# Masking the turned probabilities of sliding-window attention: one VectorE instruction into one tile instead of two into two

## The chip, the cores and the metric

One core of a Trainium2 chip runs one program. The metric is the device time of one execution, in microseconds (us); shown are the median and the spread of three executions, and one further execution that was profiled. In the profile PE is the engine of matmuls and PEld its loading of weights, DVE is VectorE, ACT is ScalarE, POOL is GpSimd and SP issues the transfers.

## What is computed

A decoder trunk of two layers, for 1024 prompt tokens and 64 sample tokens of width 1024: a gated-MLP token mixer, then grouped-query attention over a sliding window of 128 tokens with a sink per head, and behind each a SwiGLU feed-forward part. The change lies in the attention of the prompt alone:

```python
def swa_prompt(q, k, v, sinks):            # blocks of 128 queries, 16 heads, 2 key heads, 64 wide
    kk = concatenate([previous block of k, own block of k])        # 256 keys per block
    band = (kpos <= qpos) & (qpos - kpos < WINDOW)
    valid = band & ((block > 0) | (kpos >= WINDOW))
    scores = einsum('bnqkgd,bnskd->bnkgqs', qb, kk) * HEAD_DIM ** -0.5
    scores = where(valid, scores, -inf)
    probs = sink_softmax(scores, sinks)
    out = einsum('bnkgqs,bnskd->bnqkgd', probs, vv)
```

Of a query's 256 keys exactly 128 are in its window: key j of its own block if j is not behind the query, else key j of the block before. So the kernel keeps 128 scores per query, and separates the two kinds only when the probabilities meet the values.

## The kernel before

The program is one stream of matmuls with everything else beside it. The feed-forward parts and projections are products in two halves of precision: an operand is split into a high part (ACT copies it, lines 391 and 635) and a low part (DVE subtracts, lines 392 and 636), and three matmuls take the place of one (lines 629 to 631, 1000 to 1002, 1368 to 1370).

The attention stands between the first layer's feed-forward part and the output projection. It works in 32 **units**, one for a pair of heads f (0 to 7) and a pair of blocks n0 (0, 2, 4, 6). A unit goes through these steps:

- **scores** (lines 2292 to 2314): PE multiplies queries and keys (2302, 2303) into two PSUM banks; ACT copies the own block's scores into a tile `sc` (2306, 2309) and DVE writes the previous block's over it where the window wants them (2307, 2310). There are four buffers of `sc`, and five PSUM banks called `bank`.
- **softmax** (lines 2184 to 2194): POOL puts the sink beside the scores (2187), DVE finds the maximum (2188, 2189), ACT takes exponents (2191), DVE the reciprocal (2193), POOL scales (2194).
- **turn** (line 2211): PE transposes the unit's four 128x128 squares into one PSUM buffer `aux` (three of these).
- **probs** (lines 2316 to 2325): DVE multiplies the turned squares by the mask `mcT` of the own block into half of an `act` tile (2319), and then by the mask `mpT` of the previous block back into `sc` (2321). For two of the 32 units (by the bits of `K["mp"]`) ACT copies the squares and POOL masks them instead (2323, 2324).
- **weigh** (lines 2327 to 2340): PE multiplies values and probabilities into another `aux` buffer. For each of the four squares comes a matmul with the own block's values (2335), which reads the first product, and one with the previous block's (2337), which reads the second. A unit has 8 matmuls, or 6 where n0 is 0. They are float32 and use 64 of the array's 128 columns, so the profile gives them as 128*64 and shows two records for each. All other matmuls around them are 128*128. In the trace's names `aux<-act,act` of line 2335 and `aux<-sc,act` of line 2337 are these two kinds.

Between the units stand the products of the queries (lines 629 to 631, called Q below), and later the first parts of the output projection (lines 1000 to 1002, called C below), which also need the attention's rows split by lines 635 and 636 (`convert`).

Python code records the steps with due times (`flow.later`, with the delays in `K`), but that is not the last word: the tile framework is built with `schedule_with_timeline_sim=True`, and puts each engine's instructions in the order in which its own simulated timeline finds them ready. So the length and the readiness that it assumes for an instruction decide what stands beside what on every engine. On the chip each engine keeps that order and waits on semaphores.

Of the kernel before, what the change touches and what calls it, by code (L numbers as in the profile page):

```python
# [12 lines left out]
BF16 = mybir.dt.bfloat16  # L13
I32 = mybir.dt.int32
AF = mybir.ActivationFunctionType
ALU = mybir.AluOpType
# [3 lines left out]
P = 128  # L20
# [15 lines left out]
HN = 512  # L36
# [23 lines left out]
K = {'sown': 2500, 'sprobs': 8460, 'sweigh': 1107, 'xrows': 1607, 'tokw': 17761, 'var': 4147, 'centre': 4050, 'lnfin': 5018, 'mix0': 4469, 'mixc': 1659, 'mixn': 7044, 'mixt': 988, 'ln0': 1571, 'lnc': 6100, 'krow': 92, 'vrow': 2056, 'probs': 10000, 'weigh': 556, 'beg': 73, 'beg0': 0, 'ql': [159, 251], 'mp': [191, 253, 255, 255], 'ustep': 1.65, 'sat': [19, 31], 'cst0': 3015, 'cstep': 306, 'guest': [4, 7], 'lns': 47, 'sturn': 1300, 'rops': 9500, 'rstep': 550, 'zsum': 1500}  # L60
# [155 lines left out]
def trunk_kernel(ctx, tc, a):  # L216
    nc = tc.nc
    flow = Flow()
    count = [0]

    def mk(pool, shape, dt, tag, **kw):
        count[0] += 1
        return pool.tile(shape, dt, tag=tag, name=f"{tag}_{count[0]}", **kw)

    cpool = ctx.enter_context(tc.tile_pool(name="cpool", bufs=1))
# [6 lines left out]
    def act_tile(dt=F32):  # L232
        return mk(apool, [P, T], dt, "act")
# [4 lines left out]
    def bank():  # L238
        return mk(psum, [P, 512], F32, "bank", bufs=5)
# [39 lines left out]
    def tmp(shape=None, dt=F32, tag="tmp", **kw):  # L279
        return mk(ph.t, shape or [P, HN], dt, tag, **kw)  # L280
# [4 lines left out]

    pm_i = mk(cpool, [P, P], I32, "pmi")

    mcT, mpT = mk(cpool, [P, P], BF16, "mcT"), mk(cpool, [P, P], BF16, "mpT")

    def window_masks():  # L290
        m, m2 = tmp([P, P]), tmp([P, P])
# [11 lines left out]
    class Samples:  # L303
# [41 lines left out]
        def probs(self, sc):  # L345
            p4 = turn(sc)
            ptc, ptn = sc, half_quad()
            nc.vector.tensor_tensor(ptc, p4, kpS[:, None, :].to_broadcast([P, 4, P]), op=ALU.mult)
            nc.vector.tensor_tensor(ptn[:DS], p4[:DS], nwS[:DS, None, :].to_broadcast([DS, 4, P]), op=ALU.mult)
            flow.later(K["sweigh"], lambda: self.weigh(ptc, ptn))  # L350

        def weigh(self, ptc, ptn):

            halves = []
            for hb in range(2):
                ps = bank()
                for e in range(2):
                    j, out = 2 * hb + e, ps[:, e * 256:(e + 1) * 256]
                    v, vn = (t[:, 4 * hb:4 * hb + 4, :].rearrange("p b d -> p (b d)") for t in (self.cv, self.vnew))
                    nc.tensor.matmul(out, ptc[:, j, :], v, start=True, stop=False)  # L360
                    nc.tensor.matmul(out, ptn[:DS, j, :], vn, start=False, stop=True)
                own = tmp([P, P])
                for b in range(4):
                    r = slice(b * 32, (b + 1) * 32)
                    nc.scalar.activation(own[r, :].rearrange("p (e d) -> p e d", e=2),
                                         ps[r, :].rearrange("p (e b d) -> p e b d", e=2, b=4)[:, :, b, :], AF.Copy)
                halves.append(own)
            flow.pe(2000)
            W.done(self.slot)
            flow.later(K["sown"], lambda: self.features(halves))  # L370
# [1827 lines left out]
    def half_quad():  # L2198

        if not halves:  # L2200
            t = act_tile()
            halves.extend(t[:, i * HN:(i + 1) * HN] for i in range(2))
        return halves.pop(0).rearrange("p (q j) -> p q j", q=4)
# [4 lines left out]
    def turn(sc):  # L2208
        ps = aux()
        for j in range(4):  # L2210
            nc.tensor.transpose(ps[:, j * P:(j + 1) * P], sc[:, j, :], ident)
        flow.pe(440)
        return ps.rearrange("p (q j) -> p q j", q=4)
# [78 lines left out]
    def scores(f, n0):  # L2292
        kv = f // 4
        scw = quad("sc", 4)
        sc = scw[:, :, :P]
        for i in range(2):
            n = n0 + i
            ps = bank().rearrange("p (e j) -> p e j", e=2)
            k0 = max(n - 1, 0) * P
            for e in range(2):  # L2300
                q = S[f][e][:, n * P:(n + 1) * P]
                nc.tensor.matmul(ps[:, e, :], q, kk[kv][0][:, k0:k0 + 256], start=True, stop=False)
                nc.tensor.matmul(ps[:, e, :], q, kk[kv][1][:, k0:k0 + 256], start=False, stop=True)
            sv = sc[:, 2 * i:2 * i + 2, :]
            if n:
                nc.scalar.activation(sv, ps[:, :, P:], AF.Copy)
                nc.vector.copy_predicated(sv, pm_i[:, None, :].to_broadcast([P, 2, P]), ps[:, :, :P])
            else:
                nc.scalar.activation(sv, ps[:, :, :P], AF.Copy)
                nc.vector.copy_predicated(sv, pm_i[:, None, :].to_broadcast([P, 2, P]),  # L2310
                                          neg[:, None, :].to_broadcast([P, 2, P]))
        flow.pe(900)
        softmax(scw, sinkq[:, f].rearrange("p i e -> p (i e)"), 4)
        flow.later(K["probs"], lambda: probs(f, n0, sc))

    def probs(f, n0, sc):
        p4 = turn(sc)
        pc = half_quad()
        nc.vector.tensor_tensor(pc, p4, mcT[:, None, :].to_broadcast([P, 4, P]), op=ALU.mult)
        if K["mp"][n0 // 2] >> f & 1:  # L2320
            nc.vector.tensor_tensor(sc, p4, mpT[:, None, :].to_broadcast([P, 4, P]), op=ALU.mult)
        else:
            nc.scalar.activation(sc, p4, AF.Copy)
            nc.gpsimd.tensor_tensor(sc, sc, mpT[:, None, :].to_broadcast([P, 4, P]), op=ALU.mult)
        flow.later(K["weigh"], lambda: weigh(f, n0, sc, pc))

    def weigh(f, n0, pp, pc):
        kv = f // 4
# [45 lines left out]
    for st in range(4 * KD):  # L2374
        f, s = divmod(st, 4)
# [72 lines left out]
```

## Time and profile before

| | |
|---|---|
| median of three executions | 2109.6 us (2109.23 to 2111.39) |
| the profiled execution | 2105.51 us |
| its span, first to last instruction | 2103.8 us |
| mean granted TensorE clock | 0.999 |
| attention units on the trace | 1113 us (first turn) to 1294 us (last weigh) |

The page counts busy time by engine over the span; the view by windows does the same for a stretch. Records of matmuls overlap, since a new one starts before the last has ended: the pace of PE is read from the distance between starts in the timeline, not from a record's length. The view of waits names for each idle time of an engine the instruction that ended it.

### The profile page before, as it was taken

How to read it: one execution, taken by the hardware profiler on the slowest of the kernel's cores; microseconds unless marked ns; L12 is line 12 of the kernel's file. 1: busy time of each engine (PE TensorE's matmuls, PEld its weight loads, DVE VectorE, ACT ScalarE, POOL GpSimd, SP SyncE). 2: the span in 40 equal slices, each digit the busy share in tenths (PEclk: the TensorE clock that was granted, in tenths of full speed). 3: DMA queues.
4: the chain of work that ended last, by engine and by line, in shares of the span. 5: the costliest groups of instructions: out<-in, count | busy, mean ns of one | idle time of the engine just before them, and what ended most of it. 6: DMA issues, size and time to landing. Idle time of an engine off the chain costs nothing.

```text
span 2103.8 us, 29105 instructions
## 1 busy us (share of the span) xinstructions
PE 2076.8 (99%) x10890; PEld 1781.2 (85%) x10890; DVE 1357.5 (65%) x2141; ACT 1042.4 (50%) x2078; POOL 180.0 (9%) x259
## 2 busy tenths in 40 slices
PE   8999999999999999999999999999999999999998
PEld 8999888888888888888898887888888888888886
DVE  5565467665656675676767776576666666665676
ACT  6245556544444443534576665565444544344342
POOL 2422210000000000000114331110000000000000
PEclk9999999999999999999999999999999999999999
DMA  6211332332232338767442212423232323277574
GB/s 235 80 41 32 102 130 67 96 98 90 97 98 90 95 121 287 244 192 232 123 131 55 54 31 67 145 79 96 82 103 97 102 77 108 87 274 259 180 247 150
DMA packets 161312, 261.56 MB, mean 124 GB/s; under 512 B 21009, under 2 KB 86673, under 8 KB 161170
## 3 DMA queue, kind: packets, MB, share of 16 engines
q1 hardware_dynamic: 161170, 259.69, 38.0%
q8 instruction: 86, 1.41, 0.3%
q14 instruction: 56, 0.46, 0.1%
HBM read 193.42 MB, written 60.62 MB: 121 GB/s over the span
## 4 chain that ended last, share of the span: by engine, by line
PE 93%; DVE 4%; ACT 1%; DMA 1%; issue 1%; POOL 0%; SPq 0%; DVEq 0%; POOLq 0%; ACTq 0%
PE bank L1594 14%; PE bank L1368 13%; PE bank L1369 13%; PE bank L1370 13%; PE bank L629 5%; PE bank L630 5%; PE bank L631 5%; PE aux L1594 4%; PE bank L1000 3%; PE bank L1002 3%; PE bank L1001 3%; PE bank L1448 2%; PE bank L1447 2%; PE aux L1602 2%; PE aux L1101 1%; PE aux L914 1%
## 5 line engine op out<-in xcount | busy, mean ns | idle before, releaser
L1368 PE MATMUL bank<-act,act 128*128 128x512 f32 x1232 | 485.0, 394 | 1.8 <-ACT act L1776 1.8
L1369 PE MATMUL bank<-act,act 128*128 128x512 f32 x1232 | 482.3, 391 | 0.0
L1370 PE MATMUL bank<-act,act 128*128 128x512 f32 x1232 | 479.5, 389 | 0.0
L1594 PE MATMUL bank<-act,act 128*128 128x512 f32 x1452 | 341.2, 389 | 0.0
L1594 PEld LDWEIGHTS bank<-act,act 128*128 128x128 f32 x1452 | 272.4, 188 | 56.5
L392 DVE TENSOR_TENSOR act<-raw,act 128x1024 fp32r<-128x1024 f32 x186 | 228.1, 1229 | 123.2 <-ACT act L391 113.5
L391 ACT ACTIVATE act<-raw 128x1024 fp32r<-128x1024 f32 x186 | 196.5, 1058 | 207.8 <-PE bank L1448 67.5
L1370 PEld LDWEIGHTS bank<-act,act 128*128 128x128 f32 x1232 | 231.4, 188 | 48.8
L1368 PEld LDWEIGHTS bank<-act,act 128*128 128x128 f32 x1232 | 231.6, 188 | 47.8 <-ACT act L1776 2.7
L1369 PEld LDWEIGHTS bank<-act,act 128*128 128x128 f32 x1232 | 231.7, 188 | 43.2
L635 ACT ACTIVATE act<-act 128x1024 fp32r<-128x1024 f32 (+5 forms) x207 | 163.8, 837 | 178.9 <-PE bank L1594 69.8
L636 DVE TENSOR_TENSOR act<-act,act 128x1024 fp32r<-128x1024 f32 (+5 forms) x207 | 190.3, 958 | 42.0 <-ACT act L635 30.8
L629 PE MATMUL bank<-act,act 128*128 128x384 f32 (+1 forms) x624 | 208.7, 335 | 8.5 <-ACT act L522 8.5
L630 PE MATMUL bank<-act,act 128*128 128x384 f32 (+1 forms) x624 | 205.4, 330 | 0.7 <-DVE tok L973 0.7
L631 PE MATMUL bank<-act,act 128*128 128x384 f32 (+1 forms) x624 | 205.6, 330 | 0.0
L485 ACT ACTIVATE raw<-raw,vcol 128x256 f32<-128x256 f32 x352 | 151.9, 498 | 69.4 <-DMA raw<-in_f_w_up 43.8
L978 POOL TENSOR_TENSOR tok<-tok,expo 128x1 f32<-128x1 f32 (+1 forms) x63 | 39.0, 619 | 1587.5 <-DVE tok L973 1587.5
L629 PEld LDWEIGHTS bank<-act,act 128*128 128x128 f32 x624 | 118.1, 189 | 10.3 <-ACT act L522 8.5
L630 PEld LDWEIGHTS bank<-act,act 128*128 128x128 f32 x624 | 118.1, 189 | 2.0 <-issue 1.0
L631 PEld LDWEIGHTS bank<-act,act 128*128 128x128 f32 x624 | 118.0, 189 | 0.9 <-issue 0.9
L1000 PE MATMUL bank<-act,act 128*128 128x512 f32 x256 | 100.9, 397 | 1.9 <-DVE sc L339 1.5
L1001 PE MATMUL bank<-act,act 128*128 128x512 f32 x256 | 100.1, 392 | 0.0
(280 smaller groups left out, 3094.6 us busy)
## 6 DMA issues: line engine op xcount, KB each, us to landing
act<-in_f_w_down SPq DMA_DIRECT2D x90, 512.0 KB
raw<-in_f_w_gate SPq DMA_DIRECT2D x44, 512.0 KB
raw<-in_f_w_up SPq DMA_DIRECT2D x44, 512.0 KB
act<-hid_s SPq DMA_DIRECT2D x40, 512.0 KB
rows<-stream SPq DMA_DIRECT2D x24, 512.0 KB
hid_x<-rows SPq DMA_DIRECT2D x44, 256.0 KB
hid_s<-act SPq DMA_DIRECT2D x44, 256.0 KB
hid_s<-rows SPq DMA_DIRECT2D x44, 256.0 KB
```

Source lines behind the costliest of these rows:

```text
L391: nc.scalar.activation(self.hi, raw, AF.Copy)
L392: nc.vector.tensor_tensor(self.lo, raw, self.hi.bitcast(F32), op=ALU.subtract)
L629: nc.tensor.matmul(out[:, :n], h, xh[:, cs:cs + n], start=begin, stop=False)
L630: nc.tensor.matmul(out[:, :n], h, xl[:, cs:cs + n], start=False, stop=False)
L631: nc.tensor.matmul(out[:, :n], l, xh[:, cs:cs + n], start=False, stop=end)
L635: nc.scalar.activation(hi, src, AF.Copy)
L636: nc.vector.tensor_tensor(lo, src, hi.bitcast(F32), op=ALU.subtract)
L1000: nc.tensor.matmul(ps[:m, :], xh, h, start=begins and j == 0, stop=False)
L1368: nc.tensor.matmul(ps, h, xh, start=begin and k == 0, stop=False, skip_group_check=not begin)
L1369: nc.tensor.matmul(ps, h, xl, start=False, stop=False, skip_group_check=not begin)
L1370: nc.tensor.matmul(ps, l, xh, start=False, stop=k == 3, skip_group_check=not begin)
L1594: nc.tensor.matmul(ps, x, w, start=begin and e == k == 0, stop=end and e == n - 1 and k == 2, skip_group_check=adds)
```

## The change

The two masks become two halves of one tile `mcp`; `mcT` and `mpT` are views of it. In `probs`, one DVE instruction reads the turned squares twice (a broadcast over a dimension of two), multiplies them by both masks, and writes 1024 elements per partition into one `act` tile `both`. `weigh` then reads both operands from that tile. The branch with ACT and POOL is gone, and `sc` has no reader or writer behind the turn.

```diff
-    mcT, mpT = mk(cpool, [P, P], BF16, "mcT"), mk(cpool, [P, P], BF16, "mpT")
+    mcp = mk(cpool, [P, 2, P], BF16, "mcp")
+    mcT, mpT = mcp[:, 0, :], mcp[:, 1, :]
...
     def probs(f, n0, sc):
         p4 = turn(sc)
-        pc = half_quad()
-        nc.vector.tensor_tensor(pc, p4, mcT[:, None, :].to_broadcast([P, 4, P]), op=ALU.mult)
-        if K["mp"][n0 // 2] >> f & 1:
-            nc.vector.tensor_tensor(sc, p4, mpT[:, None, :].to_broadcast([P, 4, P]), op=ALU.mult)
-        else:
-            nc.scalar.activation(sc, p4, AF.Copy)
-            nc.gpsimd.tensor_tensor(sc, sc, mpT[:, None, :].to_broadcast([P, 4, P]), op=ALU.mult)
-        flow.later(K["weigh"], lambda: weigh(f, n0, sc, pc))
+        both = act_tile()[:, :2 * HN].rearrange("p (s q j) -> p s q j", s=2, q=4)
+        nc.vector.tensor_tensor(both, p4[:, None].to_broadcast([P, 2, 4, P]), mcp[:, :, None, :].to_broadcast([P, 2, 4, P]),
+                                op=ALU.mult)
+        flow.later(K["weigh"], lambda: weigh(f, n0, both[:, 1], both[:, 0]))
```

In the changed file the lines up to `probs` have a number higher by one, and those behind it a number lower by three: the new instruction is line 2320, the matmuls of weigh are lines 2332 and 2334, the turn is 2212.

The framework gives nearly all of the attention another order. Three places show how.

PE, the fourth unit (its output is `aux_9933` before and `aux_9930` after; `bank_9998` and `bank_9994` hold the same product of queries). Before:

```order
L631 MATMUL bank_9998<-act_8873,act_9522 128x384
L2335 MATMUL aux_9933<-act_9895,act_9378 64x128
L629 MATMUL bank_9998<-act_8942,act_9521 128x384
L630 MATMUL bank_9998<-act_8943,act_9521 128x384
L631 MATMUL bank_9998<-act_8942,act_9522 128x384
L629 MATMUL bank_9998<-act_8967,act_9521 128x384
L2337 MATMUL aux_9933<-sc_9683,act_9378 64x128
L2335 MATMUL aux_9933<-act_9895,act_9378 64x128
L2337 MATMUL aux_9933<-sc_9683,act_9378 64x128
L2335 MATMUL aux_9933<-act_9895,act_9378 64x128
L2337 MATMUL aux_9933<-sc_9683,act_9378 64x128
L2335 MATMUL aux_9933<-act_9895,act_9378 64x128
```

After:

```order
L632 MATMUL bank_9994<-act_8941,act_9521 128x384
L2212 MATMUL aux_9895<-ident_71,sc_9710 128x128 x4
L2332 MATMUL aux_9930<-act_9893,act_9377 64x128
L2334 MATMUL aux_9930<-act_9893,act_9377 64x128
L2332 MATMUL aux_9930<-act_9893,act_9377 64x128
L2334 MATMUL aux_9930<-act_9893,act_9377 64x128
L2332 MATMUL aux_9930<-act_9893,act_9377 64x128
L2334 MATMUL aux_9930<-act_9893,act_9377 64x128
L2332 MATMUL aux_9930<-act_9893,act_9377 64x128
L2334 MATMUL aux_9930<-act_9893,act_9377 64x128
L630 MATMUL bank_9994<-act_8966,act_9520 128x384
```

Before, one matmul of the unit (own block) goes ahead, four of the queries follow, and then come the other seven; after, the eight stand together. Over the whole order of PE the 240 matmuls of weigh stand in 46 runs before and in 30 after; before, 18 of the 32 units are cut in two (13 times into 1 and 7, five times into 3 and 3, and none is after).

DVE, near the end of the attention. Line 339 (340 after) writes a part of the samples' scores and releases a bank; lines 636 (637 after) with `act<-act` are the low parts of the conversions. Before:

```order
L636 TENSOR_TENSOR act_11766<-aux_11757,act_11766 128x256
L636 TENSOR_TENSOR act_11775<-act_10327,act_11775 128x256
L636 TENSOR_TENSOR act_11775<-act_10659,act_11775 128x256
L636 TENSOR_TENSOR act_11789<-act_9878,act_11789 128x256
L636 TENSOR_TENSOR act_11792<-act_9878,act_11792 128x64
L636 TENSOR_TENSOR act_11789<-act_9996,act_11789 128x256
L636 TENSOR_TENSOR act_11792<-act_9996,act_11792 128x64
L636 TENSOR_TENSOR act_11799<-act_10327,act_11799 128x256
L636 TENSOR_TENSOR act_11792<-act_10327,act_11792 128x64
L636 TENSOR_TENSOR act_11799<-act_10659,act_11799 128x256
L636 TENSOR_TENSOR act_11792<-act_10659,act_11792 128x64
L339 COPY_PREDICATED sc_11853<-nsi_10060,bank_11855 128x4x8
```

After:

```order
L637 TENSOR_TENSOR act_11691<-aux_11682,act_11691 128x256
L2320 TENSOR_TENSOR act_11706<-aux_11701,mcp_87 128x1024
L340 COPY_PREDICATED sc_11836<-nsi_10056,bank_11838 128x4x8
L637 TENSOR_TENSOR act_11708<-act_9876,act_11708 128x256
L637 TENSOR_TENSOR act_11711<-act_9876,act_11711 128x128
L637 TENSOR_TENSOR act_11708<-act_9992,act_11708 128x256
L637 TENSOR_TENSOR act_11711<-act_9992,act_11711 128x128
```

Line 339 stood behind all the conversions before, and now stands ahead of them; the last scores' line 2307 goes the other way, behind them.

PE, the last units but one. Each reads what DVE makes of the turn (line 2211, or 2212 after) of its own unit: `act_11958` after is made from `aux_11953`. After:

```order
L2334 MATMUL aux_11928<-act_11919,act_9377 64x128
L2212 MATMUL aux_11953<-ident_71,sc_11795 128x128 x4
L2332 MATMUL aux_11960<-act_11958,act_9377 64x128
L2334 MATMUL aux_11960<-act_11958,act_9377 64x128
L2332 MATMUL aux_11960<-act_11958,act_9377 64x128
```

Before, seven matmuls of another unit stood between these two steps:

```order
L2335 MATMUL aux_11946<-act_11936,act_9378 64x128
L2211 MATMUL aux_11971<-ident_71,sc_11812 128x128 x4
L2337 MATMUL aux_11946<-sc_11670,act_9378 64x128
L2335 MATMUL aux_11946<-act_11936,act_9378 64x128
L2337 MATMUL aux_11946<-sc_11670,act_9378 64x128
L2335 MATMUL aux_11946<-act_11936,act_9378 64x128
L2337 MATMUL aux_11946<-sc_11670,act_9378 64x128
L2335 MATMUL aux_11946<-act_11936,act_9378 64x128
L2337 MATMUL aux_11946<-sc_11670,act_9378 64x128
L2335 MATMUL aux_11978<-act_11936,act_9378 64x128
```

So after the change this one unit's weigh follows its turn directly.

## The prediction

> **What bounds the kernel.** First the page: busy time by engine, and the chain that ended last.
>
> ```profile
> PE 2076.8 (99%) x10890; PEld 1781.2 (85%) x10890; DVE 1357.5 (65%) x2141; ACT 1042.4 (50%) x2078; POOL 180.0 (9%) x259
> ...
> PE 93%; DVE 4%; ACT 1%; DMA 1%; issue 1%; POOL 0%; SPq 0%; DVEq 0%; POOLq 0%; ACTq 0%
> ```
>
> PE is busy nearly always and holds 93% of the chain. So an instruction less on DVE, ACT or POOL is worth nothing by itself. The change can move the time in two ways only: by the idle time of PE in the attention, and by the PE time that the order of its matmuls costs. The first is bounded by the view of PE's waits from 1100 to 1340 us (total, times, longest):
>
> ```profile
> PE bank L1000 <- DVE sc L339: 1.5, 1, 1.5
> PE aux L2211 <- POOL sc L2194: 1.4, 2, 0.9
> PE aux L2335 <- ACT tmp L1991: 0.8, 1, 0.8
> PE aux L2335 <- DVE act L2319: 0.7, 1, 0.7
> PE bank L1000 <- ACT act L391: 0.4, 1, 0.4
> ```
>
> These five sum to 4.8 us. That is all that shorter waits could ever bring; only the 1.5 us of line 2335 is a wait for the product that the change merges (at the 0.8 us too, which the view gives to line 1991, the matmul's real operand is line 2319's). The next view, by windows (length, then busy time of PE, PEld, DVE, ACT, POOL), shows where DVE could become the limit:
>
> ```profile
> 1120.00:1200.00 80.00, 78.39 (x626) 69.19 (x626) 59.42 (x141) 54.78 (x201) 27.38 (x40) 1.00 0.16 44
> 1260.00:1280.00 20.00, 17.80 (x185) 13.67 (x184) 19.59 (x60) 14.82 (x56) 5.24 (x6) 1.00 0.19 62
> ```
>
> Over most of the attention DVE has a quarter of its time free; from 1260 to 1280, where the conversions of the attention's rows come, it is full, and PE loses 2.2 us there.
>
> **The second way: what a visit to weigh costs PE.** The timeline of PE at the fourth unit, which is cut into one matmul and seven:
>
> ```profile
> 1130.29 0.34 PE L631 MATMUL bank<-act,act 128*128 128x384 f32 x1
> 1130.56 0.43 PE L2335 MATMUL aux<-act,act 128*64 128x128 f32 x2
> 1130.92 0.45 PE L629 MATMUL bank<-act,act 128*128 128x384 f32 x1
> ...
> 1131.38 0.35 PE L631 MATMUL bank<-act,act 128*128 128x384 f32 x1
> 1131.56 0.34 PE L629 MATMUL bank<-act,act 128*128 128x384 f32 x1
> 1131.83 0.32 PE L2337 MATMUL aux<-sc,act 128*64 128x128 f32 x1
> ...
> 1132.86 0.44 PE L630 MATMUL bank<-act,act 128*128 128x384 f32 x1
> ```
>
> Two matmuls of the queries start 0.18 us apart (1131.38, 1131.56). With one matmul of weigh between, two start 1130.92 - 1130.29 = 0.63 us apart: that visit costs 0.45 us. The other seven cost 1132.86 - 1131.56 - 0.18 = 1.12 us. Together 1.57. Against it a unit whose eight stand together:
>
> ```profile
> 1293.03 0.40 PE L1000 MATMUL bank<-act,act 128*128 128x512 f32 x1
> 1293.26 0.40 PE L1001 MATMUL bank<-act,act 128*128 128x512 f32 x1
> 1293.59 0.45 PE L2335 MATMUL aux<-act,act 128*64 128x128 f32 x4
> ...
> 1294.66 0.50 PE L1002 MATMUL bank<-act,act 128*128 128x512 f32 x1
> ```
>
> Here the starts lie 1.40 us apart where 0.23 would do: 1.17 us for the whole unit. So the cut costs 1.57 - 1.17 = **0.40 us**. From the two pieces alone: twelve more records (two per matmul) cost 1.12 - 0.45 = 0.67 us, 0.056 each, and so a visit has a fixed part of 0.45 - 0.11 = 0.34 us. Both say that PE pays for going to weigh and back, not only for the matmuls. I take 0.40, since it compares a whole unit with a cut one.
>
> The Trainium skill, page "TensorEngine Tiling (Array Packing)", section Key Properties, states that a change of tiling mode drains TensorE. By that rule the price belongs to each change between 128*128 and 128*64, whatever the neighbour; without it the price of a cut would be nothing and the gain below would shrink to the waits. The fixed 0.34 us in the rows speaks for the rule.
>
> **The change, part by part.**
>
> - *Order of PE.* The new order has the 240 matmuls of weigh in 30 visits and not in 46, since both operands come ready at once. PE does 16 visits less: 16 x 0.40 = 6.4 us (5.4 with 0.34). PE is the limit nearly everywhere here, so it counts in full, but for about one unit in the full stretch of DVE. Nothing is added on PE.
> - *DVE.* The prices, from DVE's own timeline:
>
> ```profile
> 1264.26 1.22 DVE L392 TENSOR_TENSOR act<-raw,act 128x1024 fp32r<-128x1024 f32 x1
> 1265.39 0.44 DVE L2307 COPY_PREDICATED sc<-pmi,bank 128x256 f32<-128x256 int32 x1
> ...
> 1272.28 0.68 DVE L2319 TENSOR_TENSOR act<-aux,mcT 128x512 f32<-128x512 f32 x1
> 1272.88 0.67 DVE L2321 TENSOR_TENSOR sc<-aux,mpT 128x512 f32<-128x512 f32 x1
> 1273.48 0.76 DVE L2307 COPY_PREDICATED sc<-pmi,bank 128x256 f32<-128x256 int32 x2
> ...
> 1274.47 2.62 DVE L636 TENSOR_TENSOR act<-act,act 128x256 fp32r<-128x256 f32 x10
> 1277.02 0.19 DVE L339 COPY_PREDICATED sc<-nsi,bank 128x32 f32<-128x32 int32 x1
> ```
>
>   The pair holds DVE for 1.20 us (1272.28 to 1273.48). No row has 1024 elements out of PSUM; line 392 has 1024 out of SBUF and holds DVE for 1.13 us (1264.26 to 1265.39). Bounds: 1.13, and 2.4 us if it went at half that pace. I take 1.13, since line 2319 already reads PSUM and a broadcast mask at the pace of its size. DVE then gives up 30 x 0.07 = 2.1 us and takes on 2 x 0.53 = 1.1 for the two units that ACT and POOL shared; off the path, hidden by DVE's free quarter. What ACT and POOL lose lies beside PE too.
> - *The added wait.* Weigh's first matmul needed 0.68 us of DVE before and needs 1.22 now; its second operand comes 0.06 us earlier (0.60 + 0.68 before). The whole of PE is queued behind that first matmul. In the new order I counted PE's work between each unit's turn and its weigh at the spacings above: the shortest are 0, 1.5, 1.6, 2.0, 2.1, 2.3 and 2.3 us, the rest 2.7 or more. How long DVE needs from the turn on:
>
> ```profile
> 1283.30 0.60 PE L2211 MATMUL aux<-ident,sc 128*128 128x128 f32 x4
> ...
> 1283.93 0.69 DVE L2319 TENSOR_TENSOR act<-aux,mcT 128x512 f32<-128x512 f32 x1 [0.90 <-PE aux L2211]
> ```
>
>   From the turn's first matmul 0.63 us to DVE's start, then 1.22; the turn holds PE for some 0.6 of it. So a distance of 1.3 us suffices when DVE is free. Only the unit with 0 waits for certain: **+1.3 us**, and the last one, behind lines 348 and 349, about +0.2.
> - *Waits that go.* The 0.8 and the 0.7 us of line 2335: all other units have distance enough now (-1.5). The 1.5 us of line 339: it stood behind ten conversions (2.62 us), and now stands ahead. The next late thing is line 2307 of the last scores, which has gone behind them, and whose bank the next product of the projection needs. From line 2320 of the unit ahead, DVE has to do some 12.1 us until then (conversions at 0.26 each, the rest by the rows above) and PE 11.7, so some 0.5 us stays (-1.0). One of the two waits for POOL, 0.5 us: `sc` now comes free with the turn, so the next scores run further ahead (-0.5).
> - *SP.* Two weight loads move behind more of the small shifts of line 1977. They go to tiles that are read tens of us later; I cost this at nothing.
>
> Waits: +1.5 - 3.0 = -1.5. A new order may bring waits I don't see, so I take -1.0. **Sum: -6.4 - 1.0 = -7.4 us.** Against the profiled execution (2105.5) that gives 2098.1; the executions shown have a median 4.1 us above it, and I carry the difference: 2109.6 - 7.4 = **2102.2 us**.
>
> **Rivals.**
>
> - *DVE becomes the bound.* For it: 19.59 of 20 us busy from 1260 on, and the distances of 1.5 to 2.1 us don't hold if two more instructions of 0.6 us stand ahead on DVE (then 2.5 us are needed, not 1.3). The wait for line 339 stays whole (no gain), those four units wait some 2.6 us in all, and the visits saved in the full stretch (0.8) don't count: 6.4 - 0.8 - (1.5 + 2.6) + (1.5 + 0.5) = 3.5 us gained, 2106.1. Against it: DVE's load doesn't grow.
> - *The visits cost nothing that returns.* If the fixed part were only the matmuls' start that later work makes up, just the waits change: 2108.6. Against it: two separate pieces give 0.34.
> - *Slower: the merged instruction is slow.* One mechanism: two broadcasts out of PSUM, with POOL at work beside it. A DVE row that is stretched exists, line 2052; line 2319 in the same place is not (minimum, median, maximum in ns):
>
> ```profile
> L2052 DVE TENSOR_TENSOR tmp<-tmp,act x30: 472/556/1928, 1099.6 to 1260.9; 64x384 fp32r<-64x384 f32 x21, 64x320 fp32r<-64x320 f32 x9
> ...
> L2319 DVE TENSOR_TENSOR act<-aux,mcT x32: 658/690/693, 1119.0 to 1291.6; 128x512 f32<-128x512 f32 x32
> ```
>
>   At 2.4 us each, a unit needs a distance of 2.5 us: the seven below it wait 4.4 us more, three or four in DVE's full stretch add 4.2, and DVE's extra 32 x 1.2 us would take most of its free quarter, which I put at 2.0 us of further waits: -7.4 + 10.6 = 3.2 us slower, 2112.8. It outweighs the gain from about 2 us on. Line 2319's narrow spread speaks against it.
>
> **How the numbers follow.** What a measurement of this kernel can tell from no change is about 0.2%, 4.2 us. The forecast (gain of 4.2 to 11) gets 0.75; DVE as the bound 0.14 and visits without a price 0.06, both within 0.2%; slower 0.05. So faster 0.75, same 0.20, slower 0.05. The range goes down to a gain of 11 us (16 x 0.42 and nearly all waits gone), 2098.6, and up to a gain of 2 (between the first two rivals), 2107.6.
>
> **What would show it.** In the profile of the changed kernel: weigh's records in runs of 12 or 16, at 1.17 us a unit with no lone pair; the merged instruction at 1.22 us with little spread; PE's waits in the attention at 3 to 5 us, the largest at the last unit but one and at the first product behind the conversions; the stage from the first turn to the first product of the second half shorter by about 7 us, and everything behind it moved by as much. A merged instruction over 2 us, or waits over 8 us, would make the prediction wrong.

## The result, and the profile after

| | before | after |
|---|---|---|
| median of six runs, us | 2109.4 | 2098.1 |
| ratio, with its 95% interval | | 0.9949 (0.9939 to 0.9959) |
| the same kernel again, in a later round of runs | 2108.7 | 2096.4 |
| ratio there | | 0.9945 (0.9932 to 0.9959) |
| profiled execution, us (span) | 2105.5 (2103.8) | 2098.6 (2096.9) |

The change saves 10.8 us (8.6 to 12.9). 0.9949 of the 2109.6 us from which the prediction starts is 2098.8: faster, 3.4 us beyond the forecast and just inside the low end of the range (2098.6). The interval reaches past that end, so it is in part luck that the time fell inside.

The page of the changed kernel, busy time by engine and the chain that ended last:

```profile
PE 2068.0 (99%) x10890; PEld 1779.8 (85%) x10890; DVE 1358.3 (65%) x2111; ACT 1041.7 (50%) x2076; POOL 176.2 (8%) x257
...
PE 91%; DVE 5%; ACT 2%; DMA 1%; issue 1%; POOL 0%; SPq 0%; DVEq 0%; POOLq 0%; ACTq 0%
```

PE has the same 10890 records and is busy 8.8 us less. DVE has 30 instructions less and no less work (1357.5 before). So the gain isn't fewer busy microseconds on DVE; the same matmuls cost PE less. Where? The view of one line's instructions gives the first and the last start of each. First two lines of the kernel before: the turn, and the first matmul of the part behind the attention.

```profile
L2211 PE MATMUL aux<-ident,sc x136: 270/273/331, 1113.8 to 1290.4; 128*128 128x128 f32 x136
...
L1205 PE MATMUL bank<-act,ones x18: 387/394/398, 1300.7 to 1386.4; 128*128 128x512 f32 x18
```

The same two of the changed kernel:

```profile
L2212 PE MATMUL aux<-ident,sc x136: 270/273/330, 1116.8 to 1283.8; 128*128 128x128 f32 x136
...
L1206 PE MATMUL bank<-act,ones x18: 387/394/398, 1294.1 to 1379.8; 128*128 128x512 f32 x18
```

From the first turn to line 1205 (1206) it was 1300.7 - 1113.8 = 187.0 us (by the unrounded starts) and is 177.3: **-9.7 us**, for the same 1466 PE records. This stretch is called the stage from here on. Behind it everything moves alike: the last start of that line stands 85.7 us after its first in both. The two profiled executions differ by 6.9 us only, since this one of the changed kernel reached its first turn 3.0 us later (first scores at 1107.1, not 1104.8), by what lies ahead of the stage. One part of that is a stretch at half the granted clock (the third number from the end), which the profiled execution of before did not have there:

```profile
1044.25:1047.60 3.35, 3.35 (x15) 3.35 (x14) 2.82 (x5) 1.37 (x3) 0.45 (x1) 0.50 0.45 156
```

Such a stretch of 3.4 us costs up to 1.7 us where PE is the limit (an estimate: half of it). Another 0.7 us is a longer wait of the first turn itself. The stage is the better measure: in both kernels the clock was 1.00 all through it, and it agrees with the timed runs.

PE's waits from 1100 to 1340 us in the changed kernel (total, times, longest):

```profile
PE aux L2332 <- DVE act L2320: 3.0, 2, 1.5
PE aux L2212 <- POOL sc L2195: 1.6, 1, 1.6
PE bank L1001 <- DVE sc L2308: 1.0, 1, 1.0
PE bank L1001 <- ACT act L392: 0.4, 1, 0.4
```

6.0 us in all, 5.2 before (the five rows that the prediction quotes, 4.8, and some small ones). One of them, for POOL at the first turn, lies ahead of the stage in both kernels (before, then after):

```profile
1113.77 0.66 PE L2211 MATMUL aux<-ident,sc 128*128 128x128 f32 x4 [0.86 <-POOL sc L2194]
1116.81 0.66 PE L2212 MATMUL aux<-ident,sc 128*128 128x128 f32 x4 [1.55 <-POOL sc L2195]
```

Inside the stage the waits are 4.3 us before and 4.4 after. They have not become less; all of the 9.7 us comes from PE's own time, the stage less its waits: 182.7 us before, 172.9 after. One unit of the weighing, between two matmuls of the queries, from PE's timeline:

```profile
1230.53 0.34 PE L631 MATMUL bank<-act,act 128*128 128x384 f32 x1
1230.80 0.45 PE L2332 MATMUL aux<-act,act 128*64 128x128 f32 x4
1231.07 0.40 PE L2334 MATMUL aux<-act,act 128*64 128x128 f32 x4
1231.28 0.44 PE L2332 MATMUL aux<-act,act 128*64 128x128 f32 x4
1231.50 0.44 PE L2334 MATMUL aux<-act,act 128*64 128x128 f32 x4
1231.87 0.44 PE L632 MATMUL bank<-act,act 128*128 128x384 f32 x1
1232.15 0.34 PE L630 MATMUL bank<-act,act 128*128 128x384 f32 x1
```

The sixteen records stand together. Look at the last two rows: the first matmul behind the visit takes 0.28 us to the next start (1231.87 to 1232.15), where matmuls of the queries are 0.18 apart. The prediction priced a visit up to the start of the matmul behind it and so left out 0.10 us. The row that it passed over in the kernel before says the same:

```profile
1131.20 0.34 PE L630 MATMUL bank<-act,act 128*128 128x384 f32 x1
...
1133.14 0.34 PE L631 MATMUL bank<-act,act 128*128 128x384 f32 x1
```

With these ends, the cut unit cost (1131.20 - 1130.29 - 2 x 0.18) + (1133.14 - 1131.56 - 2 x 0.18) = 0.55 + 1.22 = 1.77 us, and the whole one costs 1232.15 - 1230.53 - 2 x 0.18 = 1.26. A cut costs **0.51 us** and not 0.40.

The merged instruction, in the view of its line (minimum, median, maximum in ns), and the two stretches that the prediction showed (length, then busy time of PE, PEld, DVE, ACT, POOL). The second is taken 10 us earlier, since the same work now comes that much earlier:

```profile
L2320 DVE TENSOR_TENSOR act<-aux,mcp x32: 1194/1218/1225, 1122.1 to 1285.0; 128x1024 f32<-128x1024 f32 x32
```

```profile
1120.00:1200.00 80.00, 80.00 (x721) 74.74 (x720) 65.83 (x139) 59.27 (x216) 29.20 (x45) 1.00 0.16 40
1250.00:1270.00 20.00, 18.49 (x199) 15.11 (x198) 19.15 (x51) 16.66 (x65) 6.15 (x8) 1.00 0.22 62
```

1.22 us with little spread. DVE's full stretch (19.59 of 20 before) has not gone, it has moved: 19.15 of 20, with 1.5 us lost by PE. In the first 80 us PE is busy throughout.

### The profile page after: what moved, and what is told of

The parts are those of the page before. It is cut to its first block, busy times and chain, and to the rows that moved or that the text cites. A ratio compares the mean times of both kernels' runs of the same rounds, so it can differ in the third digit from the quotient of the medians.

```text
span 2096.9 us, 29073 instructions
## 1 busy us (share of the span) xinstructions
PE 2068.0 (99%) x10890; PEld 1779.8 (85%) x10890; DVE 1358.3 (65%) x2111; ACT 1041.7 (50%) x2076; POOL 176.2 (8%) x257
## 4 chain that ended last, share of the span: by engine, by line
PE 91%; DVE 5%; ACT 2%; DMA 1%; issue 1%; POOL 0%; SPq 0%; DVEq 0%; POOLq 0%; ACTq 0%
PE bank L1595 14%; PE bank L1369 13%; PE bank L1370 13%; PE bank L1371 13%; PE bank L630 4%; PE bank L631 4%; PE bank L632 4%; PE aux L1595 4%; PE bank L1001 3%; PE bank L1003 3%; PE bank L1002 3%; PE bank L1449 2%; PE bank L1448 2%; PE aux L1603 2%; PE aux L1102 1%
## 5 line engine op out<-in xcount | busy, mean ns | idle before, releaser
L630 PEld LDWEIGHTS bank<-act,act 128*128 128x128 f32 x624 | 118.5, 190 | 10.2 <-ACT act L523 9.3
```

Source lines behind the costliest of these rows:

```text
L630: nc.tensor.matmul(out[:, :n], h, xh[:, cs:cs + n], start=begin, stop=False)
```

## The experiments

The theory: **the gain is the order of PE**, 16 visits to the weighing fewer. Rival 1: the score tile comes free earlier and GpSimd leaves the path. Rival 2: VectorE's work is what counts. Times are medians; ratios go against the kernel before, run on the same chip. The changed kernel stands at 0.9949 and 0.9945. Some profiled executions below have stretches at half clock inside the stage; for them, PE's own time is the stage less its waits and less half of the time at 0.50. That half is an estimate and a little high: in such a stretch matmuls of 256 columns start 0.21 us apart (1218.37 to 1218.59 in the run with work beside), and 0.12 outside.

### The order of the weighing alone

```
-        for i in range(2):
+        for i in (1, 0):
...
-                nc.tensor.matmul(out, vtok[:, n, ...], pc[:, j, :], start=True, stop=(n == 0))
                 if n:
-                    nc.tensor.matmul(out, vtok[:, n - 1, ...], pp[:, j, :], start=False, stop=True)
+                    nc.tensor.matmul(out, vtok[:, n - 1, ...], pp[:, j, :], start=True, stop=False)
+                nc.tensor.matmul(out, vtok[:, n, ...], pc[:, j, :], start=(n == 0), stop=True)
```

> The kernel before the change, both masked forms by two instructions into two tiles as before; only the weighing takes its eight matmuls in another order: of each pair the one with the previous block's form first, and the second block ahead of the first. So its first matmul needs the product that comes last, and nothing can be put between. TensorE goes to the weighing 30 times in this program. The output is the same. Theory (fewer visits): most of the gain is there, -6 to -10 us, 2099 to 2104 us, and TensorE waits 1 to 3 us more for the later product than in the changed kernel. Rival 1 (score tile free earlier) and rival 2 (VectorE does less): nothing of either is changed, so 2108 to 2111 us.

Measured: 2101.1 us, 0.9958 (0.9945 to 0.9970). Four fifths of the gain (0.42 of 0.51%) come without touching the products or their tiles. Its stage, first turn to line 1205, is 181.1 us, -5.9, although its waits are longer, as the theory expected (6.2 us in the stage, for 4.4 in the changed kernel), and although 3.4 us of it ran at half clock (from 1117.8 on). PE's own time is 173.2 us: all but 0.3 us of the gain in it is there. PE's waits in the attention, the four longest totals:

```profile
PE aux L2336 <- DVE sc L2321: 3.4, 5, 1.6
PE aux L2211 <- POOL sc L2194: 1.6, 1, 1.6
PE bank L1000 <- DVE sc L2307: 0.9, 1, 0.9
PE bank L2302 <- DVE sc L2307: 0.8, 1, 0.8
```

The weighing now waits for the second of the two products (line 2321, the first row), five times.

### Two instructions into one tile

```
-        nc.vector.tensor_tensor(both, p4[:, None].to_broadcast([P, 2, 4, P]), mcp[:, :, None, :]...
+        nc.vector.tensor_tensor(both[:, 0], p4, mcT[:, None, :].to_broadcast([P, 4, P]), op=ALU.mult)
+        nc.vector.tensor_tensor(both[:, 1], p4, mpT[:, None, :].to_broadcast([P, 4, P]), op=ALU.mult)
```

> The changed kernel, but the one tile is filled by two VectorE instructions of 512 columns, as before the change; the output is the same. TensorE goes to the weighing 46 times in this program, as before the change, and 30 times in the changed one. Theory (the time is saved by fewer visits of TensorE to the weighing, about 0.5 us each): the gain is gone, 2107 to 2110 us. Rival 1 (the time is saved because the score tile comes free earlier and GpSimd is out of the path): the gain stays, 2098 to 2100 us. Rival 2 (VectorE does less): VectorE has 32 x 1.2 us of the pair again, so the gain is gone here too; this run doesn't tell rival 2 from the theory.

Measured: 2105.8 us, 0.9982 (0.9972 to 0.9992), between the two expectations. Its stage is 184.5 us, -2.4, although 3.4 us of it, from 1224 on, ran at half clock; with 46 visits as before, two thirds of the gain are gone. What is left, 2 to 6 us, is not the visits. So rival 1 is not nothing, or another order by itself brought a few microseconds. The next run asks for the tile alone.

### The second product in a tile of its own

```
+        pp = act_tile()[:, :HN].rearrange("p (q j) -> p q j", q=4)
...
-            nc.vector.tensor_tensor(sc, p4, mpT[:, None, :].to_broadcast([P, 4, P]), op=ALU.mult)
+            nc.vector.tensor_tensor(pp, p4, mpT[:, None, :].to_broadcast([P, 4, P]), op=ALU.mult)
```

(ScalarE and GpSimd write to `pp` too, and the weighing reads it.)

> The kernel before the change, still with two masked products by two instructions into two tiles (and ScalarE with GpSimd for the two units that they took); only the second product goes into a tile of its own and not into the score tile. TensorE goes to the weighing 46 times. The output is the same. Theory (the visits are all): no change, 2108 to 2111 us. Rival 1 (the score tile that comes free with the turn is worth something by itself, as the run with two instructions and one tile suggests): 2 to 5 us faster than before, 2104 to 2107 us.

Measured: 2107.3 us, 0.9996 (0.9987 to 1.0005). A score tile that comes free with the turn is worth 0.8 us by this (at most 2.7) and can't be told from nothing. Rival 1 falls as the main cause. Whether the run before gained more than this one stays open: the intervals overlap a little, and PE's own time in the stage is 181.7 us here, 180.3 there and 182.7 before.

### Two instructions, no cuts

One tile and two instructions, as two runs ago, with the weighing in the order of the first experiment.

> The changed kernel with two VectorE instructions into the one tile instead of one, and the weighing in the order that needs the later product first, so that nothing is put between: TensorE goes to the weighing 31 times, and the score tile comes free with the turn, as in the changed kernel. The output is the same. What is left of the change is only that one instruction is two. Theory (visits and the free score tile are all, the merged instruction itself saves 0.07 us of VectorE each): 2097 to 2101 us. Rival (the merged instruction itself is worth something): 2101 to 2106 us, between the run with the weighing's order alone (2101) and the one with two instructions and one tile (2106).

Measured: 2101.1 us, 0.9955 (0.9943 to 0.9968). Against the run with two instructions, one tile and 46 visits (0.9982) it differs in nothing but the weighing's order: -0.27%, 5.7 us, for 15 visits. The run can't be told from the changed kernel, whose interval overlaps: by the ratios, that the two products come by one instruction is worth 1 to 2 us by itself. In the profiles nothing of it is left: the stage is 178.8 us, for 177.3 in the changed kernel, and this stretch at half clock accounts for up to 1.7 us of it:

```profile
1261.90:1265.20 3.30, 3.30 (x46) 2.83 (x44) 3.06 (x9) 2.41 (x9) 0.66 (x2) 0.50 0.18 65
```

The change works because one instruction delivers both operands at once, and not because one instruction is cheaper than two.

### Cutting the weighing again

The changed kernel, with the weighing's two blocks put into the order 3 us apart:

```
+        part(0)
+        flow.later(3000, rest)
```

(`part(i)` is the loop's body for one block; `rest` does the second block and the copy.)

> The changed kernel with one instruction and one tile; only the weighing is cut in two parts by its first and its second block, the second put into the order 3 us later, so that TensorE goes to the weighing 46 times, as before the change. The output is the same. Theory (visits, about 0.5 us each): 16 x 0.5 = 8 us slower than the changed kernel, 2104 to 2108 us. Rivals 1 and 2 (score tile, VectorE): both stay as in the changed kernel, 2097 to 2100 us.

Measured: 2105.7 us, 0.9982 (0.9974 to 0.9991): 7 us slower than the changed kernel. Cutting alone takes back most of the gain, partly by a lower clock (below). The price of such a cut, from this kernel's timeline (matmuls of the queries of 320 columns stand 0.15 apart here):

```profile
1165.93 0.31 PE L630 MATMUL bank<-act,act 128*128 128x320 f32 x1
1166.17 0.45 PE L2332 MATMUL aux<-act,act 128*64 128x128 f32 x4
1166.44 0.40 PE L2334 MATMUL aux<-act,act 128*64 128x128 f32 x4
1166.77 0.42 PE L631 MATMUL bank<-act,act 128*128 128x320 f32 x1
1167.02 0.31 PE L632 MATMUL bank<-act,act 128*128 128x320 f32 x1
```

1167.02 - 1165.93 - 2 x 0.15 = 0.79 us for half a unit; two halves less a whole, 1.58 - 1.26 = 0.32 us. That is less than the 0.51 of before, because the cut is even. In the first visit here the four records of a row cover both column halves; a lone matmul of before, with its odd partner in the other visit, leaves a half empty. That this makes the difference of 0.19 us is argued from the rows, not run by itself. The Trainium skill, page "TensorEngine Tiling (Array Packing)", section Key Properties, has tiles operate independently, so that different ones can run in parallel; by that rule a lone half should cost what a pair costs. The rows agree: in the cut unit of the prediction records stand in pairs 0.01 us apart (1131.83 and 1131.84), and one pair follows the other by some 0.11.

14 to 16 cuts at 0.32 are 5 us of the 7. In the profiled execution PE's own time is 178.8 us, 5.9 more than in the changed kernel, and the waits are 2.2 us less. The rest is a lower clock. The longest stretch (the third number from the end is the granted clock):

```profile
1219.00:1225.60 6.60, 6.60 (x28) 4.64 (x28) 1.67 (x2) 2.23 (x7) 0.38 (x2) 0.50 0.14 31
```

There is a second one of 3.4 us at 1263. In the changed kernel's stage the clock was 1.00. Together they cost up to 5.1 us, in this one execution. Over all eleven the mean clock is 0.9967, for 0.9980 in the changed kernel; at 1.5 us for each 0.001 (the last section has that figure) this is some 2 us.

### More work on VectorE

Three runs add to the changed kernel: the merged instruction twice; two instructions of 512 columns behind it into a tile that nobody reads; one of 256 columns. The edit of the second:

```
+        nc.vector.tensor_tensor(spare, both[:, 0], both[:, 1], op=ALU.mult)
+        nc.vector.tensor_tensor(spare, both[:, 0], both[:, 1], op=ALU.mult)
```

> The changed kernel with the merged instruction issued twice, the second over the first's result: VectorE has 32 x 1.1 us = 36 us more work, and the weighing waits for the second. TensorE goes to the weighing 29 times. The output is the same. Theory (TensorE sets the time, VectorE lies beside it): only the waits of the weighing grow, by about 1.1 us in the few units where little stands between turn and weighing, and the softmax waits a little: +2 to +8 us against the changed kernel, 2100 to 2106 us. Rival 2 (VectorE's work sets the time): +20 to +36 us, 2118 to 2134 us.

> The changed kernel with two more VectorE instructions of 512 columns behind each merged one, into a tile that nobody reads: 32 x 1.2 = 38 us more work on VectorE, as much as in the run with the merged instruction twice (which was 35 us slower than the changed kernel), but the weighing doesn't wait for it. TensorE goes to the weighing 30 times, as in the changed kernel. The output is the same. Theory A (what cost 35 us there is VectorE's time itself, since its queue runs in order and its idle time is not free): 20 to 38 us slower than the changed kernel, 2118 to 2136 us. Theory B (as the prediction had it, VectorE lies beside TensorE; the 35 us came from the later product): 0 to 8 us slower, 2098 to 2106 us.

> The changed kernel with one VectorE instruction of 256 columns behind each merged one, into a tile that nobody reads: 32 x 0.4 = 13 us more work on VectorE, a third of the run with the work beside (which cost 13 us). 30 visits; the output is the same. Theory (VectorE has some slack: a small addition is hidden, only a large one is paid): 0 to 2 us slower than the changed kernel. Rival (each microsecond of VectorE in this stage costs a third of a microsecond, from the first on): 4 us slower.

Measured: twice, 2132.9 us, 1.0105 (1.0092 to 1.0119); beside, 2111.7, 1.0010 (1.0001 to 1.0019); small, 2100.1, 0.9966 (0.9953 to 0.9979). Against the changed kernel that is 35, 13 and 4 us, for 39, 49 and 14 us of added work. The theory's figure for the first was far off, and neither A nor B was right for the second. Twice, in DVE's timeline:

```profile
1142.43 1.19 DVE L2320 TENSOR_TENSOR act<-aux,mcp 128x1024 f32<-128x1024 f32 x1
1143.54 0.47 DVE L2053 TENSOR_TENSOR tmp<-tmp,act 64x320 fp32r<-64x320 f32 x1
1143.94 0.50 DVE L2311 COPY_PREDICATED_SCALAR sc<-pmi,neg 128x256 f32 x1
1144.33 0.43 DVE L2308 COPY_PREDICATED sc<-pmi,bank 128x256 f32<-128x256 int32 x1
1144.66 1.21 DVE L2322 TENSOR_TENSOR act<-aux,mcp 128x1024 f32<-128x1024 f32 x1
```

The second does not follow the first: three other instructions stand between, and the product that the weighing needs comes 2.2 us later, not 1.1. PE's longest waits there:

```profile
PE aux L2334 <- DVE act L2322: 10.3, 7, 4.3
PE bank L337 <- DVE sc L2308: 3.0, 1, 3.0
```

With the work beside, the same wait makes 7.7 us in seven times, and in the stretch where DVE had its free quarter it has none:

```profile
1120.00:1200.00 80.00, 78.51 (x700) 73.12 (x698) 79.08 (x163) 58.01 (x207) 29.85 (x41) 1.00 0.16 40
```

79.08 of 80 us. With the small addition PE's first two waits are

```profile
PE aux L2334 <- DVE act L2321: 3.4, 2, 1.9
PE bank L1001 <- DVE sc L2309: 1.7, 1, 1.7
```

against 3.0 and 1.0: not a new wait, the same two grown. So both sizes beside are paid at about the same rate, 13/49 and 4/14, some 0.27 us for each, from small on, which is near the third of the last rival. About half of it comes through the clock: of the 17.1 us that the stage of the large one is longer in the profile, up to 10.2 are half clock, and of the 3.8 us of the small one up to 1.7. Without that it is some 0.15 us for each. DVE's free quarter does not hide what is added in front of something that PE waits for: DVE takes its instructions in their order, as its rows show.

### Still fewer visits

Two units weighed at once, into the two halves of one tile, the later unit first:

```
+        held.append((f, n0, both[:, 1], both[:, 0]))
+        if len(held) == 2:
+            two = [held.pop(0) for _ in range(2)]
+            flow.later(K["weigh"], lambda: weigh(two))
```

(`weigh(two)` goes through both units and writes each into its half of one `aux` tile.) The second run of the three puts that 2.5 us behind the second turn (`'weigh': 2500`), the third takes the changed kernel with `'weigh': 0`.

> The changed kernel, but the weighing takes two units at once, into two halves of one tile, the later unit first: TensorE goes to the weighing 18 times, not 30. The output is the same. Theory (each visit costs 0.5 to 0.6 us): 12 x 0.55 = 6.6 us less, less 0 to 4 us of new waits (scores and copies stand differently): 2091 to 2098 us. Rival (VectorE or the waits bound the stage, so fewer visits bring nothing more): 2098 to 2104 us.

> The run that weighs two units at once, with the weighing put into the order 2.5 us after the second turn and not 0.6 us: 17 visits. The output is the same. Theory (that run had 18 visits but lost what they save, by waits that came from where its products and scores stood, 10.0 us against 5.7 in the changed kernel, and a granted clock of 0.996): with the weighing later the wait for the product (2.3 us of it) goes, 2096 to 2100 us. Rival (fewer visits than 30 bring nothing whatever the waits): 2100 to 2104 us.

> The changed kernel with the weighing put into the order at once behind the turn (delay 0, not 0.6 us): 27 visits, three fewer. The output is the same. Theory (a visit costs 0.5 to 0.6 us): 1.5 us less for the visits, and 0 to 3 us more waits for the merged instruction where less stands between: 2096 to 2100 us, hard to tell from the changed kernel's 2098. Rival (the later product is what limits): 2100 to 2106 us.

Measured: 2101.5 us, 0.9968 (0.9955 to 0.9980) with 18 visits; 2106.3, 0.9977 (0.9968 to 0.9986) with 17; 2102.4, 0.9962 (0.9950 to 0.9975) with 27. None beats the changed kernel. The first and the third came at the figure that was given to the rival, the second beyond it. PE's waits, two units at once:

```profile
PE aux L2212 <- POOL sc L2195: 3.4, 2, 2.2
PE bank L630 <- ACT tmp L1992: 3.0, 1, 3.0
PE aux L2344 <- DVE act L2322: 2.4, 2, 2.2
```

and later, where one wait alone takes what the visits saved:

```profile
PE bank L1001 <- ACT act L392: 4.8, 1, 4.8
```

The mean clock of these two profiled runs is 0.997 and 0.992, for 0.998 in the changed kernel. Waits and clock take back what the visits save: with 18 visits PE's own time is 169.6 us, 3.3 less than with 30, but the waits are 4.1 us longer and up to 3.4 us go to half clock. In the run with 17 visits half clock takes up to 12.0 us. What a visit below 30 is worth by itself is not shown: too much else is changed in these orders.

### The changed kernel again

> The changed kernel again, beside the run with the small addition, so that the two stand on the same chip: 2097 to 2100 us, 0.994 to 0.996 of before. If it comes out at 2101 or more, the three microseconds between it and the two runs without cuts (two instructions) mean nothing.

Measured: 2096.4 us, 0.9945 (0.9932 to 0.9959). Its stage is 177.2 us (177.3 in the other profile), with the same two waits for the merged product, 3.0 us in all. The gain stands in a second round, and the stage repeats to 0.1 us. By the test set here the 3 us to the two runs without cuts mean something; but in the stages up to 1.7 us of them is half clock in both runs, and in the run with the order alone 1.8 us are longer waits, so they are no gain of the merged instruction itself.

Over all runs PE's own time in the stage goes with the visits: 178.8 to 182.7 us in the four runs with 46 of them, 172.1 to 173.2 in those with 28 to 31, whatever else was changed. With 27 visits it is 174.4, with 18 169.6 and with 17 172.2; in the first and the last of these three some more PE work of another kind (5 and 18 records) fell into the stage.

## Why the prediction came out as it did

**Order of PE, -6.4: right in kind, too small.** The visits, 46 before and 30 after, are the cause: the order alone gives most of the gain, and cutting again costs 7 us, some 5 of them by the cuts. The step that was mis-sized is the price: "0.40, since it compares a whole unit with a cut one". Both were measured only up to the start of the matmul behind, and that one is late too: 0.51 with it, 16 x 0.51 = 8.2. The trace of the stage, counted from each start to the next, gives more: the 480 records of the weighing 38.5 us before and 32.3 after (-6.3), the step into a visit 16 x 0.095 = 1.5 less, the first matmul behind it 1.8 less, since 18 visits before went back to the queries, where it costs 0.10, and only 3 do now; most (22, before 19) go on to a turn, where it costs 0.06. That makes -9.6, or 0.60 for a visit. The 0.09 between 0.51 and 0.60 I can't lay to single units.

**DVE: the price right, the cover not.** The merged instruction takes 1.22 us and the next starts 1.11 to 1.14 behind it (1142.43 to 1143.54 above), for 1.13 predicted. That DVE's work is "off the path, hidden by DVE's free quarter" is wrong: added work cost 0.27 of itself, some 0.15 without the clock. It did no harm here, because the change leaves DVE's work within 1 us of what it was.

**The added wait, +1.5: half of it.** The waits for the merged product are 3.0 us. The unit with distance 0 waits 1.5 us, about the size given (+1.3). A second wait of 1.5 us was not foreseen:

```profile
1257.62 1.08 PE L335 MATMUL bank<-act,act 128*32 128x128 f32 x32
1260.21 0.45 PE L2332 MATMUL aux<-act,act 128*64 128x128 f32 x4 [1.51 <-DVE act L2320]
...
1281.88 0.45 PE L2332 MATMUL aux<-act,act 128*64 128x128 f32 x4 [1.48 <-DVE act L2320]
```

It stands behind the samples' scores, at one of the distances that I had counted at 1.5 us or more and took for enough. That distance is long (the unit's turn starts at 1255.63), but DVE was not free:

```profile
1257.65 1.37 DVE L393 TENSOR_TENSOR act<-raw,act 128x1024 fp32r<-128x1024 f32 x1 [0.45 <-ACT act L392]
1258.94 1.21 DVE L2320 TENSOR_TENSOR act<-aux,mcp 128x1024 f32<-128x1024 f32 x1
```

This is DVE's full stretch, where the first rival expected such waits. The last unit's 0.2 did not show.

**Waits that go, -3.0: nearly.** The wait of line 339 moved to line 2308, as worked out, but stayed at 1.0 us where 0.5 was expected (1.5 before). The 0.8 and 0.7 of line 2335 went, and so did the one wait for POOL of 0.5 us inside the stage. That the view's total for POOL did not fall (1.4 and 1.6) is the first turn, ahead of the stage. In all -1.0 was taken; measured was +0.8 in the whole view and +0.1 in the stage. The errors on the visits (3.2 us too little gain) and on the waits (1.1 us too much in the stage) partly cancel; -9.6 + 0.1 leaves 0.2 of the stage's -9.7 without a place.

**The base.** The profiled execution of before was a quick one, 2.6 us below the fastest timed run; it had no stretch at half clock before its last microseconds. To take the differences from it, but the time from the median of the runs, was right: from the two profiled executions alone the gain would be 6.9 us.

**Rivals.** DVE as the bound came in one unit only, the second wait above (DVE is at 65.83 of 80 and, in its full stretch, 19.15 of 20); visits without a price fell with the first experiment, and the slow merged instruction with 1.22 us. Doubled, it does what that rival said of 2.4 us, and worse: 35 us slower than the changed kernel where 10.6 was worked out, since the second one also stands behind what the order put between, and since up to 10.2 us of its stage go to half clock.

## What to carry to other kernels

When PE is busy 99% of the time, look at what order its matmuls stand in: each change to a narrow tile and back costs it 0.3 to 0.6 us here, and the scheduler made such changes in 18 of 32 units where the two operands came one after the other. Let both operands of an accumulating pair come ready at once, or let the first matmul be the one that needs the later of the two: the second is an edit of a few lines and gives four fifths of it. Measure the price of a visit to where the old rhythm is back, not to the start of the first matmul behind it. Before comparing stages, look where the granted clock was halved in each.

## What was not expected of the hardware

The granted clock is not 1.00 throughout, although only one core runs, and it accounts for part of what the slower runs lose. In all fourteen traces it is 1.00 or 0.50 (a window that holds both shows a value between), and up to the last microseconds of a run the half comes in stretches of 3.4 us or two or four times that. The run with work beside, around its wait of 2.1 us (at 1215 to 1217):

```profile
1214.70:1218.10 3.40, 1.29 (x8) 0.95 (x7) 3.37 (x7) 1.58 (x9) 0.97 (x2) 1.00 0.28 65
1218.20:1231.70 13.50, 13.50 (x50) 9.17 (x50) 7.97 (x16) 7.14 (x30) 4.01 (x5) 0.50 0.20 41
```

13.5 us at 0.50 are worth up to 6.8 us. The Trainium skill, page "TensorE: Matmul & The Clock Gate", section "What's actually happening", has the array's clock halved after an idle window of about 3.4 us. The half clock is seen here, behind a wait of 2.1 us. But a wait of 3.0 us in the run with the weighing sooner left it at 1.00:

```profile
1250.00:1260.00 10.00, 7.60 (x53) 6.01 (x51) 8.62 (x21) 6.69 (x24) 2.61 (x4) 1.00 0.13 31
1260.00:1270.00 10.00, 8.58 (x140) 6.99 (x140) 9.51 (x20) 6.65 (x28) 1.56 (x3) 1.00 0.16 54
```

and the half clock of the run with the cut weighing, from 1219 on, came without a wait. In that run and in three others (two instructions into one tile, the small addition, the weighing sooner) it came during or within 1.2 us behind the samples' matmuls of lines 361 and 362, which start some 0.3 us apart; but the changed kernel passed the same lines at 1.00. What sets it stays open. The mean clock over a run follows the waits roughly: 0.998 in the changed kernel's runs, 0.993 with the merged instruction twice, and within one kernel a run is about 1.5 us longer for each 0.001 that it is lower.
